# Output gates of the mLSTM heads computed as Strassen pairs in the gate stage, in a one-core diffusion step

## The chip, the cores and the metric

The kernel runs on one core of a Trainium2 chip. The metric is the device time of one execution in microseconds (us). Engines are named as in the profile: PE is the matrix engine (PEld its weight loads), DVE the vector engine, ACT the scalar engine, POOL the general one, SP the one whose queue issues most loads.

## The reference

One step of a layer for 256 context tokens and 1024 latent tokens, all fp32, model width 1024, four mLSTM heads of 128:

```python
u = rmsnorm(x, g_norm1) * (1 + sc1) + sh1
proj = u @ w_in
xp, su, sv, q, k, v, o_pre, gate_pre, br_pre = jnp.split(proj, points, axis=-1)
y_a = pool_branch(xp, w_pool, pool_scale, grid)
y_b = sgu_branch(su, sv, g_sgu, w_sgu, b_sgu)
y_c, C_out, n_out, m_out = mlstm_branch(q, k, v, o_pre, gate_pre, ...)
branches = jnp.einsum('btrc,rcd->btrd', ys, w_branch)
gates = jax.nn.sigmoid(br_pre).reshape(B, T, N_BRANCH, D_MODEL)
merged = jnp.sum(gates * branches, axis=2)
x = x + gt1 * (merged @ w_out)
...
# at the end of mlstm_branch: h is the sum of both scans' rows, per head
h = h * lax.rsqrt(jnp.mean(h * h, axis=-1, keepdims=True) + EPS) * g_mlstm
y = jax.nn.sigmoid(o_pre) * h
```

After that come the feed-forward block (`relu(...)^2`) and a last RMSNorm. What matters here is `sigmoid(o_pre)`, the output gate of the heads: 512 columns of `w_in`, one block of 128 for each head, over 1280 tokens.

## The kernel before

All 1280 tokens lie along the free axis, in three groups: 512, 512 and 256 (`GROUPS`; the last holds the context). An fp32 product is made from three matmuls on split operands: hi·hi, hi·lo and lo·hi. So a plain projection of one block of 128 columns (`proj`, `dense`) takes 8 k-tiles x 3 = 24 matmuls for each group, 72 in all: 48 of 128x512 and 24 of 128x256 (L123 to L125).

The larger products of the layer are made in pairs of column blocks by a Strassen scheme (`Pair`, L910 to L912): 7 products of four k-tiles for the 1024 latent tokens, which are read as sums prepared once (`us`), and plain products for the context group. `GatePair` does it for the 24 column blocks of the branches' gates, in 12 pairs: its results get a sigmoid (`done`, L992) and are stored to DRAM (`scr_g`), where the merge reads them back.

The stages, in order of the code: adaLN and norm; gating scans; the four heads (about 80 to 450 us); the SGU's `sv` and the pooling windows (450 to 576); gate pairs (576 to 877); merge (877 to 1150); output projection, feed-forward, last norm.

A head (`head(h, kT, vT, qT)`) first transposes k and v (tk, tv), forms the states of both scans (kv, L596; L607), and then goes over the three groups. In each: `st` (k·q, L627) and `rb` (rows of the gating broadcast to all partitions, L631) on PE; for each of the two directions DVE adds masks (L635), ACT takes Exp (L637, L643) and DVE multiplies (L638, L645) to the weights w and e; `pv` multiplies them with v and the state (L654, L656); ACT and DVE normalise (L659 to L663) and ACT squares (L664); POOL takes the power -0.5 (L130), ACT scales (L670), PE transposes to `th` (L671), DVE writes `yc` (L673) and it is stored to DRAM (`scr_yc`). At the first group of each head, the output gate's projection `p_o` is made for all three groups (L669) and evicted on ACT by a sigmoid into `so` (L617).

A scheduler sets the order of the instructions on each engine from its own model of the time; instructions of different heads and of the later `sv` projections (L698 to L702, in blocks of 24 matmuls of 128x256 for each 128 tokens) are interleaved with a head's chain. PSUM tiles of projections come from one ring of three (`mm`), those of attention from one of five (`sd`). Weights of a projection are loaded raw, cast to hi on ACT (L93) and split to lo on DVE or POOL (L94).

After each gate pair, up to six pieces of the second modulation (`mod_piece`, 64 in all, on DVE, POOL and DMA; L541) are inserted: pair n may bring the count to 6n.

The merge reads the rows of one branch after the other (`yr`, order SGU, pool, mLSTM), splits them to hi and lo (ACT, DVE), and multiplies with `w_branch` (pb, L1070 to L1072); DVE multiplies with the gate and adds up (L1074 to L1077).

Of the kernel before, what the change touches and what calls it, by code (L numbers as in the profile page):

```python
# [7 lines left out]
F32 = mybir.dt.float32  # L8
# [40 lines left out]
def hybrid_step(  # L49
# [503 lines left out]
    vaug = z[:, 1280:2570].rearrange("p (c t) -> p c t", t=129)  # L553
    vs = z[:, 2570:5150].rearrange("p (c d t) -> p c d t", d=2, t=129)
    S = z[:, 5150:7730].rearrange("p (c d t) -> p c d t", d=2, t=129)
    so = z[:, 7730:9010]
    hn2 = [z[:, 9010 + i * 512 : 9522 + i * 512].rearrange("p (c t) -> p c t", t=P) for i in range(2)]

    def proj(idx, name, evict, eng=V, w=None, groups=range(3)):
        w = w or load_w(w_in[idx], name, eng=eng)  # L560
        for g in groups:
            ps = ps_mm(f"p_{name}{g}")
            dense(ps, w, uT, g)
            evict(g, ps)
# [10 lines left out]
    def head(h, kT, vT, qT):  # L575
# [36 lines left out]
            V.scalar_tensor_tensor(fin[:, d, :], S[:, nx, d, :], dc(nx, d), kv(nx, d), ALU.mult, ALU.add)  # L612
        A.dma_start(st_out[h], fin)

        def ev_o(g, ps):
            t0, n = GROUPS[g]
            A.activation(so[:, t0 : t0 + n], ps[:, :n], AF.Sigmoid)  # L617

        ssq = small([P, 16], f"ssq{h}")
        for g in range(3):  # L620
            t0, n = GROUPS[g]
            c0, ncn = t0 // P, n // P
            hn = hn2[(3 * h + g) % 2]
            st = ps_sd(f"st{h}_{g}")
            for c in range(ncn):
                s = slice(c * P, (c + 1) * P)
                PE.matmul(st[:, s], kT[g][:, s], qT[g][:, s], start=True, stop=True)  # L627
            pw, qw = [], []
            for d in range(2):
                rb = ps_sd(f"rb{h}_{g}_{d}")  # L630
                PE.matmul(rb[:, :n], selr[:, d * 4 + h : d * 4 + h + 1].to_broadcast([100, P]), rhl[g][0:100, :n], start=True, stop=True)  # L631
                w = tmp(f"w{h}_{g}_{d}")
                for c in range(ncn):
                    s = slice(c * P, (c + 1) * P)
                    V.scalar_tensor_tensor(  # L635
                        w[:, s], rb[:, s], GC[:, c0 + c, d * 4 + h : d * 4 + h + 1], masks[d], ALU.add, ALU.add)
                A.activation(w[:, :n], w[:, :n], AF.Exp)  # L637
                V.tensor_tensor(w[:, :n], w[:, :n], st[:, :n], ALU.mult)  # L638
                pw.append(w)
                e = tmp(f"e{h}_{g}_{d}")  # L640
                for c in range(ncn):
                    s = slice(c * P, (c + 1) * P)
                    A.activation(  # L643
                        e[:, s], rb[:, s], AF.Exp, bias=mpb[:, d * 4 + h, c0 + c : c0 + c + 1], scale=1.0)
                V.tensor_tensor(e[:, :n], e[:, :n], qT[g][:, :n], ALU.mult)  # L645
                qw.append(e)
            for cl in range(ncn):
                c = c0 + cl
                s = slice(cl * P, (cl + 1) * P)
                pv = ps_sd(f"pv{h}_{c}")  # L650
                pvv = pv[:, 0:258].rearrange("p (d t) -> p d t", t=129)
                for d in range(2):
                    inter = not (c == 8 and d == 0) and not (c == 9 and d == 1)
                    PE.matmul(pvv[:, d, :], pw[d][:, s], vaug[:, c, :], start=True, stop=not inter)  # L654
                    if inter:
                        PE.matmul(pvv[:, d, :], qw[d][:, s], S[:, c, d, :], start=False, stop=True)  # L656
                den = small([P, 2, 1], f"den{h}_{c}")
                em = EM[:, c, :].rearrange("p (d h) -> p d h", d=2)[:, :, h]
                A.activation(den[:, :, 0], pvv[:, :, P], AF.Abs)  # L659
                V.tensor_tensor(den[:, :, 0], den[:, :, 0], em, ALU.max)  # L660
                V.reciprocal(den, den)
                A.activation(hn[:, cl, :], pvv[:, 0, 0:P], AF.Copy, scale=den[:, 0, :])
                V.scalar_tensor_tensor(hn[:, cl, :], pvv[:, 1, 0:P], den[:, 1, :], hn[:, cl, :], ALU.mult, ALU.add)  # L663
                A.activation(vs[:, c, 0, 0:P], hn[:, cl, :], AF.Square, accum_out=ssq[:, c : c + 1])  # L664
            r = rstd_of(ssq[:, c0 : c0 + ncn], ncn, f"h{h}_{g}")
            if g == 0:
                proj(I_O + h, f"o{h}", ev_o)
            ps = ps_sd(f"th{h}_{g}")
            for cl in range(ncn):  # L669
                A.activation(hn[:, cl, :], hn[:, cl, :], AF.Copy, scale=r[:, cl : cl + 1])  # L670
                PE.transpose(ps[:, cl * P : (cl + 1) * P], hn[:, cl, :], ident)  # L671
            yc = tmp(f"yc{h}_{g}")
            V.scalar_tensor_tensor(  # L673
                yc[:, :n], ps[:, :n], ccol[:, C_GM + h : C_GM + h + 1], so[:, t0 : t0 + n], ALU.mult, ALU.mult)
            SP.dma_start(scr_yc[h, :, t0 : t0 + n], yc[:, :n])

    qkv = head_proj(0)
# [308 lines left out]

    ORDER = (1, 0, 2)
    scr_g = [[dp.tile([P, T], F32, name=f"scr_g{r}_{d}") for d in range(KT)] for r in range(3)]

    class GatePair(Pair):  # L990
        def done(self, t):
# [2 lines left out]
        def context_done(self, t, ps):  # L994
            A.activation(t, ps, AF.Sigmoid)

        def store(self, r, d):
            for f, (t1, t2) in enumerate(((self.a1, self.a2), (self.b1, self.b2))):
                dst = scr_g[r][d + f]
                A.dma_start(dst[:, 0:512], t1)  # L1000
                A.dma_start(dst[:, 512:1024], t2)
                A.dma_start(dst[:, 1024:1280], self.hc[:, f * 256 : f * 256 + 256])

    for kk in range(4):
        us["B11", kk], us["B21", kk], us["B22", kk] = uT[kk][0], uT[kk + 4][0], uT[kk + 4][1]
    NGP = 3 * KT // 2
    gates = {}

    def gate_pair(n):
        r, d = ORDER[n // 4], n % 4 * 2  # L1010
        i = I_BR + r * KT + d
        odd = n % 2
        gates[n] = GatePair(
            f"g{n}", n, (w_in[i], w_in[i + 1]), 8 if odd else 0, (4, 5, 6, 7) if odd else (14, 15, 18, 19), us, [uT[k][2] for k in range(KT)])
# [11 lines left out]
    for n in range(NGP):  # L1026
        if n not in gates:
            gate_pair(n)
            gates[n].begin()
            gates[n].contexts()  # L1030
        gates[n].rest()
        gates[n].store(ORDER[n // 4], n % 4 * 2)
        del gates[n]
        while n > 0 and piece < 64 and piece < 6 * n:
            mod_piece(piece, zs((12, 13, 16, 17)[piece % 4]))
            piece += 1

# [7 lines left out]
    for ri, r in enumerate(ORDER):  # L1045
        scr = (scr_ya, scr_yb, scr_yc)[r]
        ys = [[] for _ in range(4)]
        for g in range(3):
            for kc in range(4):
                t0, n = GROUPS[g]  # L1050
                raw = tmp2(f"yr{r}_{kc}_{g}")
                SP.dma_start(raw[:, :n], scr[kc, :, t0 : t0 + n])
                hi, lo = split_part(f"y{r}_{kc}", g)
                A.copy(hi, raw[:, :n])
                V.tensor_tensor(lo, raw[:, :n], hi.bitcast(F32), ALU.subtract)
                ys[kc].append((hi, lo))
# [499 lines left out]
```

## Time and profile before

| | |
|---|---|
| median of three runs | 1944.16 us (1943.91 to 1946.34) |
| profiled execution, its own time | 1943.31 us |
| its span | 1941.3 us |
| PE busy | 1908.4 us (98%) |
| DVE, ACT, POOL busy | 1287.9, 856.7, 382.1 us |
| mean granted clock of PE | 0.996 |

The span is from the first to the last instruction; 2.0 us of the execution lie around it. PE is near full from beginning to end, so a group's busy time on another engine says little by itself; what is to be looked for is where PE waits, and what stands on PE between two steps of a chain on the other engines.

### The profile page before, as it was taken

How to read it: one execution, taken by the hardware profiler on the slowest of the kernel's cores; microseconds unless marked ns; L12 is line 12 of the kernel's file. 1: busy time of each engine (PE TensorE's matmuls, PEld its weight loads, DVE VectorE, ACT ScalarE, POOL GpSimd, SP SyncE). 2: the span in 40 equal slices, each digit the busy share in tenths (PEclk: the TensorE clock that was granted, in tenths of full speed). 3: DMA queues.
4: the chain of work that ended last, by engine and by line, in shares of the span. 5: the costliest groups of instructions: out<-in, count | busy, mean ns of one | idle time of the engine just before them, and what ended most of it. 6: DMA issues, size and time to landing. Idle time of an engine off the chain costs nothing.

```text
span 1941.3 us, 28162 instructions
## 1 busy us (share of the span) xinstructions
PE 1908.4 (98%) x10166; PEld 1632.5 (84%) x10166; DVE 1287.9 (66%) x2200; ACT 856.7 (44%) x1760; POOL 382.1 (20%) x381
## 2 busy tenths in 40 slices
PE   8999999999999999999999999999999999999998
PEld 5878888998788888888888888888888888888886
DVE  6574443447759899875675599887876655754665
ACT  6444454653243333343123375555454544443443
POOL 1100001108202424230000005554431210000003
PEclk9999999999999999999999999999999999999999
DMA  9210111012635445459532435777774596654444
GB/s 370 77 60 33 45 38 39 28 57 68 204 125 168 151 151 161 157 195 328 164 103 98 151 121 200 275 263 264 250 256 139 193 335 203 210 168 152 165 133 160
DMA packets 149318, 313.33 MB, mean 161 GB/s; under 512 B 17550, under 2 KB 40818, under 8 KB 147130
## 3 DMA queue, kind: packets, MB, share of 16 engines
q1 hardware_dynamic: 107354, 220.73, 34.6%
q0 software_dynamic: 15520, 57.75, 7.8%
q10 hardware_dynamic: 26304, 33.04, 4.7%
q8 instruction: 80, 1.31, 0.3%
q14 instruction: 60, 0.49, 0.1%
HBM read 217.59 MB, written 93.36 MB: 160 GB/s over the span
## 4 chain that ended last, share of the span: by engine, by line
PE 87%; DVE 6%; ACT 2%; issue 2%; DMA 2%; POOL 1%; SPq 0%; ACTq 0%; POOLq 0%; DVEq 0%
PE w L1423 6%; PE w L1424 6%; PE w L1425 6%; PE fT L912 3%; PE fT L910 3%; PE fT L911 3%; PE pb L1071 3%; PE pb L1070 3%; PE pb L1072 3%; PE fB L911 2%; PE fB L910 2%; PE fB L912 2%; PE fT_g L912 2%; PE fT_g L910 2%; PE fT_g L911 2%; PE po L1190 2%
## 5 line engine op out<-in xcount | busy, mean ns | idle before, releaser
L1262 POOL TENSOR_TENSOR z<-z 128x512 f32<-128x512 f32 x64 | 100.6, 1572 | 119.6 <-DMA z<-in_w_ff 110.1
L967 DVE TENSOR_TENSOR z<-z 128x512 f32<-128x512 f32 x112 | 94.2, 841 | 2.5
L547 POOL PARTITION_ALL_REDUCE acc<-acc x16 | 54.4, 3435 | 183.4 <-DVE acc L541 114.3
L541 DVE SCALAR_TENSOR_TENSOR acc<-z,scond,acc 128x512 f32<-128x512 f32 x112 | 84.6, 803 | 0.1
L1377 POOL TENSOR_TENSOR rs_y<-rs_y,neghalf 128x1 f32<-128x1 f32 x10 | 9.7, 967 | 332.2 <-DVE rs_y L1376 332.1
L1228 ACT ACTIVATE z<-z 128x512 f32<-128x512 f32 x64 | 40.5, 632 | 75.7 <-DVE z L976 38.4
L992 ACT ACTIVATE z<-z 128x512 f32<-128x512 f32 x48 | 30.3, 632 | 54.2 <-DVE z L976 20.6
L130 POOL TENSOR_TENSOR rs_h<-rs_h,neghalf 128x4 f32<-128x4 f32 (+1 forms) x12 | 10.9, 909 | 200.0 <-DVE rs_h L129 199.8
L673 DVE SCALAR_TENSOR_TENSOR yc<-th,ccol,z 128x512 f32<-128x512 f32 (+1 forms) x12 | 7.9, 661 | 58.4 <-PE th L671 58.4
L1076 DVE TENSOR_TENSOR sg<-pb,sg 128x512 f32<-128x512 f32 (+1 forms) x48 | 28.8, 601 | 26.6 <-PE pb L1072 26.4
L901 ACT CAST hi_wb<-raw_wb 128x512 fp32r<-128x512 f32 x24 | 14.7, 620 | 64.0 <-PE pb L1071 37.9
L1229 ACT ACTIVATE z<-z 128x512 f32<-128x512 f32 x64 | 40.3, 629 | 1.1
L1191 DVE TENSOR_TENSOR po<-po,gt 128x512 f32<-128x512 f32 (+1 forms) x24 | 14.6, 609 | 35.6 <-PE po L1190 31.2
L548 POOL TENSOR_TENSOR acc<-acc,bt 1x512 f32<-1x512 f32 x16 | 26.2, 1651 | 59.1 <-issue 59.1
L1253 POOL DMA_DIRECT2D scr_s<-x x48 | 26.3, 550 | 52.4 <-DVE x L1247 46.6
L758 POOL TENSOR_TENSOR z<-z 128x1024 f32<-128x1024 f32 (+13 forms) x20 | 33.6, 1702 | 7.7 <-ACT z L742 5.4
L1194 ACT ACTIVATE po<-z 128x512 f32<-128x512 f32 (+1 forms) x24 | 12.7, 530 | 48.6 <-DVE z L1193 34.3
L607 DVE SCALAR_TENSOR_TENSOR z<-z,dmb,kv 128x129 f32<-128x129 f32 x56 | 16.6, 345 | 21.8 <-PE kv L596 21.3
L1077 DVE TENSOR_TENSOR z<-z,sg 128x512 f32<-128x512 f32 (+1 forms) x48 | 28.7, 602 | 1.2
L660 DVE TENSOR_TENSOR den<-den,gcol 128x2 f32<-128x2 f32 x40 | 6.2, 160 | 31.0 <-ACT den L659 29.9
L130 POOL TENSOR_TENSOR rs_f<-rs_f,neghalf 128x4 f32<-128x4 f32 (+1 forms) x3 | 3.3, 1092 | 116.9 <-DVE rs_f L129 116.9
L654 PE MATMUL pv<-z,w 128*128 128x129 f32 x160 | 25.1, 275 | 0.9 <-DVE w L638 0.9
(5142 smaller groups left out, 7274.1 us busy)
## 6 DMA issues: line engine op xcount, KB each, us to landing
z<-in_w_ff SPq DMA_DIRECT2D x64, 512.0 KB, 5.3
z<-in_w_ada SPq DMA_DIRECT2D x64, 256.0 KB, 3.4
scr_t<-z POOLq DMA_DIRECT2D x16, 1024.0 KB, 4.3
z<-in_w_in SPq DMA_DIRECT2D x24, 512.0 KB, 4.3
scr_g<-z ACTq DMA_DIRECT2D x48, 256.0 KB, 2.0
sg<-scr_g SPq DMA_DIRECT2D x48, 256.0 KB, 4.5
scr_h<-z ACTq DMA_DIRECT2D x48, 256.0 KB, 3.5
scr_s<-x POOLq DMA_DIRECT2D x48, 256.0 KB, 3.8
```

Of the source, the lines that this page charges most:

```text
L541: V.scalar_tensor_tensor(acc[j], raw, scond[:, k, j : j + 1], acc[j], ALU.mult, ALU.add)
L910: PE.matmul(ps, whi[:, s], ahi, start=first and k == ks[0], stop=False)
L911: PE.matmul(ps, whi[:, s], alo, start=False, stop=False)
L912: PE.matmul(ps, wlo[:, s], ahi, start=False, stop=end and k == ks[-1])
L967: V.tensor_tensor(out, x, y, op)
L1070: PE.matmul(pb[:, :n], whi[:, s], yh, start=kc == 0, stop=False)
L1071: PE.matmul(pb[:, :n], whi[:, s], yl, start=False, stop=False)
L1072: PE.matmul(pb[:, :n], wlo[:, s], yh, start=False, stop=kc == 3)
L1262: G.tensor_tensor(out, x, y, ALU.subtract)
L1423: PE.matmul(banks[j], h_[:, s], rh, start=fp == 0, stop=False)
L1424: PE.matmul(banks[j], l_[:, s], rh, start=False, stop=False)
L1425: PE.matmul(banks[j], h_[:, s], rl, start=False, stop=fp == NFP - 1)
```

## The change

The projection of the output gates leaves the heads. Their four column blocks are made as two further `GatePair`s, numbers 12 and 13, after the 12 of the branches, with the same sigmoid and a store to DRAM (`scr_o`). In the heads `yc` is now only scaled by `g_mlstm`, on ACT instead of DVE. Where the merge reads the rows of the last branch (r = 2, mLSTM), it loads the gate too and DVE multiplies it in ahead of the split. The pieces of modulation go five to a pair instead of six.

```diff
-    so = z[:, 7730:9010]
...
-        def ev_o(g, ps):
-            t0, n = GROUPS[g]
-            A.activation(so[:, t0 : t0 + n], ps[:, :n], AF.Sigmoid)
...
             r = rstd_of(ssq[:, c0 : c0 + ncn], ncn, f"h{h}_{g}")
-            if g == 0:
-                proj(I_O + h, f"o{h}", ev_o)
...
             yc = tmp(f"yc{h}_{g}")
-            V.scalar_tensor_tensor(
-                yc[:, :n], ps[:, :n], ccol[:, C_GM + h : C_GM + h + 1], so[:, t0 : t0 + n], ALU.mult, ALU.mult)
+            A.activation(yc[:, :n], ps[:, :n], AF.Copy, scale=ccol[:, C_GM + h : C_GM + h + 1])
...
+    scr_o = [dp.tile([P, T], F32, name=f"scr_o{h}") for h in range(H)]
...
-        def store(self, r, d):
+        def store(self, dsts):
...
-                dst = scr_g[r][d + f]
+                dst = dsts[f]
...
-    NGP = 3 * KT // 2
+    GATES = [(I_BR + r * KT + d, scr_g[r][d : d + 2]) for r in ORDER for d in range(0, KT, 2)]
+    GATES += [(I_O + h, scr_o[h : h + 2]) for h in range(0, H, 2)]
+    NGP = len(GATES)
...
-        while n > 0 and piece < 64 and piece < 6 * n:
+        while n > 0 and piece < 64 and piece < 5 * n:
...
+                if r == 2:
+                    so = tmp2(f"so{kc}_{g}")
+                    SP.dma_start(so[:, :n], scr_o[kc][:, t0 : t0 + n])
+                    V.tensor_tensor(raw[:, :n], raw[:, :n], so[:, :n], ALU.mult)
```

The code behind it is the same, but the scheduler's order in the heads is not. Below are three places in head 2. In a row stand the line, the operation, what it writes and reads, the shape; names carry head and group (`rb2_2_0`: head 2, group 2, direction 0; `pv2_8`: head 2, block of tokens 8) and a running number.

PE around the second transposition and the last group, before. Between the first row of `sv0_3` and the last shown of `sv0_4` stand 40 more of the two.

```order
L671 MATMUL th2_1_2990<-cst_78,z_76 128x128
L627 MATMUL st2_2_3002<-kq2_2362 128x128 x2
L631 MATMUL rb2_2_0_3005<-rhl2_1167,selr_1171 128x256
L631 MATMUL rb2_2_1_3016<-rhl2_1167,selr_1171 128x256
L671 MATMUL th2_1_2990<-cst_78,z_76 128x128 x3
L698 MATMUL sv0_3_3856<-hi_sv0_0_3761,u0h0_384 128x256
...
L700 MATMUL sv0_4_3884<-lo_sv0_1_3768,u5h1_827 128x256
L654 MATMUL pv2_8_3027<-z_76,w2_2_0_3007 128x129
L654 MATMUL pv2_9_3038<-z_76,w2_2_0_3007 128x129
L656 MATMUL pv2_9_3038<-z_76,e2_2_0_3012 128x129
```

The same place after:

```order
L664 MATMUL th2_1_2738<-cst_78,z_76 128x128
L622 MATMUL st2_2_2750<-kq2_2194 128x128 x2
L626 MATMUL rb2_2_0_2753<-rhl2_1167,selr_1171 128x256
L626 MATMUL rb2_2_1_2764<-rhl2_1167,selr_1171 128x256
L664 MATMUL th2_1_2738<-cst_78,z_76 128x128 x3
L649 MATMUL pv2_8_2775<-z_76,w2_2_0_2755 128x129
L649 MATMUL pv2_9_2786<-z_76,w2_2_0_2755 128x129
L651 MATMUL pv2_9_2786<-z_76,e2_2_0_2760 128x129
L649 MATMUL pv2_8_2775<-z_76,w2_2_1_2766 128x129
L649 MATMUL pv2_9_2786<-z_76,w2_2_1_2766 128x129
L651 MATMUL pv2_8_2775<-z_76,e2_2_1_2771 128x129
L690 MATMUL sv1_0_3727<-hi_sv1_0_3717,u0h0_384 128x256
```

The 42 `sv` matmuls between rb and pv are gone, and `sv1_0`, one block of 24, stands between pv and the next th. At groups 0 and 1 of head 2 likewise one block of 24 is left on each side of pv (`sv0_6` to `sv0_9`), where 34 to 40 matmuls of `p_q`, `p_o` and `sv` stood.

ACT between the normalisation of head 2's group 1 and its scaling, before:

```order
L662 ACTIVATE z_76<-pv2_7_2975,den2_7_2980 128x128
L664 ACTIVATE z_76,ssq2_2721<-z_76 128x128
L701 COPY vn1_3799<-sv0_1_3800 128x256
L664 ACTIVATE z_76,ssq2_2721<-z_76 128x128
L702 ACTIVATE sv0_1_3800,vsq_3758<-sv0_1_3800 128x256
L664 ACTIVATE z_76,ssq2_2721<-z_76 128x128 x2
L670 ACTIVATE z_76<-z_76,rs_h2_1_2987 128x128 x4
```

And after, with the first rows of what follows:

```order
L657 ACTIVATE z_76<-pv2_7_2723,den2_7_2728 128x128
L659 ACTIVATE z_76,ssq2_2553<-z_76 128x128
L93 CAST hi_sv1_1_3723<-raw_sv1_1_3721 128x1024
L659 ACTIVATE z_76,ssq2_2553<-z_76 128x128 x3
L93 CAST hi_xp3_4017<-raw_xp3_4015 128x1024
L663 ACTIVATE z_76<-z_76,rs_h2_1_2735 128x128 x4
L666 ACTIVATE yc2_1_2747<-th2_1_2738,ccol_74 128x512
L632 ACTIVATE w2_2_0_2755<-w2_2_0_2755 128x256
```

Two casts of weights stand among the Squares instead of an eviction of `sv`, and `yc` (L666) stands ahead of the next group's Exp (L632).

POOL in head 2, before:

```order
L130 TENSOR_TENSOR rs_h2_0_2805<-rs_h2_0_2805,neghalf_81 128x4
L94 TENSOR_TENSOR lo_sv1_0_4054<-raw_sv1_0_4051,hi_sv1_0_4053 128x1024
L130 TENSOR_TENSOR rs_h2_1_2987<-rs_h2_1_2987,neghalf_81 128x4
L130 TENSOR_TENSOR rs_h2_2_3049<-rs_h2_2_3049,neghalf_81 128x2
L94 TENSOR_TENSOR lo_sv1_1_4060<-raw_sv1_1_4057,hi_sv1_1_4059 128x1024
```

And after:

```order
L130 TENSOR_TENSOR rs_h1_2_2183<-rs_h1_2_2183,neghalf_81 128x2
L130 TENSOR_TENSOR rs_h2_0_2637<-rs_h2_0_2637,neghalf_81 128x4
L94 TENSOR_TENSOR lo_sv1_1_3724<-raw_sv1_1_3721,hi_sv1_1_3723 128x1024
L130 TENSOR_TENSOR rs_h2_1_2735<-rs_h2_1_2735,neghalf_81 128x4
L130 TENSOR_TENSOR rs_h2_2_2797<-rs_h2_2_2797,neghalf_81 128x2
```

The split of `sv1_1` stands ahead of the power of group 1, where the split of `sv1_0` stood.

More of the change, by code (lines that the diff above doesn't have):

```diff
@@ L1005, in hybrid_step @@
         us["B11", kk], us["B21", kk], us["B22", kk] = uT[kk][0], uT[kk + 4][0], uT[kk + 4][1]
-    NGP = 3 * KT // 2
     gates = {}
+    GATES = [(I_BR + r * KT + d, scr_g[r][d : d + 2]) for r in ORDER for d in range(0, KT, 2)]
+    GATES += [(I_O + h, scr_o[h : h + 2]) for h in range(0, H, 2)]
+    NGP = len(GATES)
     def gate_pair(n):
-        r, d = ORDER[n // 4], n % 4 * 2
-        i = I_BR + r * KT + d
+        i = GATES[n][0]
         odd = n % 2
@@ L1031, in hybrid_step @@
         gates[n].rest()
-        gates[n].store(ORDER[n // 4], n % 4 * 2)
+        gates[n].store(GATES[n][1])
         del gates[n]
-        while n > 0 and piece < 64 and piece < 6 * n:
+        while n > 0 and piece < 64 and piece < 5 * n:
             mod_piece(piece, zs((12, 13, 16, 17)[piece % 4]))
```

## The prediction

> **What bounds the kernel now.** I read the page first (engine totals, the chain), then PE's waits, then windows by stage, then single stretches of the head stage.
>
> ```profile
> span 1941.3 us, 28162 instructions
> PE 1908.4 (98%) x10166; PEld 1632.5 (84%) x10166; DVE 1287.9 (66%) x2200; ACT 856.7 (44%) x1760; POOL 382.1 (20%) x381
> PE 87%; DVE 6%; ACT 2%; issue 2%; DMA 2%; POOL 1%; SPq 0%; ACTq 0%; POOLq 0%; DVEq 0%
> ```
>
> PE is busy for 98% of the span and is 87% of the chain that ended last; only 33 us of the span are not its own. So a change is worth what it takes from or adds to PE's instruction stream, plus every stall that it opens or closes in that stream.
>
> ```profile
> 140.00:450.00 310.00, 307.15 (x2049) 280.00 (x2048) 134.05 (x391) 161.56 (x470) 30.41 (x27) 1.00 0.13 42
> 575.90:877.00 301.10, 298.08 (x1571) 256.62 (x1571) 259.92 (x371) 113.45 (x208) 98.21 (x60) 1.00 0.51 166
> 877.00:1150.00 273.00, 273.00 (x1451) 235.93 (x1450) 175.71 (x320) 89.94 (x183) 10.08 (x16) 1.00 0.47 157
> ```
>
> Columns: length of the stretch, busy PE, PEld, DVE, ACT, POOL, granted clock, DMA share, GB/s. The three are the head stage, the gate pairs and the merge. PE fills each (2.9, 3.0 and 0 us short). In the head stage that is not because attention is short of dependencies: PE is kept busy by projections standing between an attention step and the next. In the gate stage DVE is the next engine (260 of 301); in the merge it has 97 us free.
>
> ```profile
> PE fT_g L912 <- DVE s_g7l L893: 1.7, 1, 1.7
> PE sv L698 <- ACT sv L702: 1.2, 1, 1.2
> PE p_xp L123 <- DVE mt L842: 1.1, 1, 1.1
> PE p_k L123 <- ACT kT L349: 0.7, 1, 0.7
> PE p_k L123 <- ACT z L617: 0.7, 1, 0.7
> ```
>
> These are the waits in PE's list that the change could touch (total, times, longest).
>
> **PE's arithmetic.**
>
> ```profile
> 100.55:114.33 13.78, 13.78 (x72) 11.84 (x72) 0.00 (x0) 1.00 0.28 91
> 177.08:185.72 8.64, 8.64 (x38) 6.95 (x38) 0.00 (x0) 1.00 0.16 63
> ```
>
> First row: one head's whole output-gate projection on PE, 72 matmuls in 13.78 us (48 of 128x512, 24 of 128x256). Second: 38 of 128x512 in 8.64 us, so 0.227 each; then a 128x256 takes (13.78 - 48 x 0.227)/24 = 0.12. Removed: four heads, 192 wide and 96 narrow. Added: two pairs; a pair is 7 products of 12 wide matmuls plus 48 narrow ones, so 168 wide and 96 narrow. Net -24 x 0.227 = **-5.4 us**. Cross-check: 12 pairs in 298.08 us are 24.84 each, against 2 x 13.78 = 27.56 for two heads the old way, 2 x 2.72 = 5.4. Since PE is full in both places, this term is the surest of the sum.
>
> **The cover that goes.** Between two attention steps PE waits for a chain. Chain A: from the first rb matmul through masks, Exp and multiply to w and e, which pv reads. Chain B: from the last pv through the normalisation, Squares, POOL's power and the scaling to the th transposes.
>
> ```profile
> 240.78 0.71 PE L631 MATMUL rb<-rhl,selr 100*128 100x512 f32 x2
> 243.36 0.68 DVE L638 TENSOR_TENSOR w<-w,st 128x512 f32<-128x512 f32 x1
> 245.70 0.69 DVE L645 TENSOR_TENSOR e<-e,qT 128x512 f32<-128x512 f32 x1 [0.27 <-ACT e L643]
> 432.64 0.48 PE L631 MATMUL rb<-rhl,selr 100*128 100x256 f32 x2
> 434.46 0.42 DVE L638 TENSOR_TENSOR w<-w,st 128x256 f32<-128x256 f32 x1
> ```
>
> Chain A is 244.04 - 240.78 = 3.3 us to the first w (5.6 to the last e) for a 512-token group, and 2.2 for the 256-token one.
>
> ```profile
> 193.15:196.89 3.74, 3.74 (x34) 3.73 (x33) 2.24 (x9) 1.78 (x7) 0.00 (x0) 1.00 0.23 26
> 196.89:200.51 3.62, 3.62 (x18) 2.99 (x17) 1.43 (x7) 1.88 (x12) 1.02 (x1) 1.00 0.39 136
> 290.29:293.50 3.21, 3.21 (x15) 2.63 (x15) 1.21 (x7) 1.57 (x9) 0.70 (x1) 1.00 0.59 163
> 352.60:356.99 4.39, 3.17 (x27) 2.96 (x26) 1.82 (x11) 3.02 (x16) 1.01 (x1) 1.00 0.06 15
> 354.00 0.40 ACT L701 COPY vn<-sv 128x256 f32<-128x256 f32 x1
> 354.56 0.41 ACT L702 ACTIVATE sv<-sv 128x256 f32<-128x256 f32 x1
> 355.24 0.33 ACT L664 ACTIVATE z<-z 128x128 f32<-128x128 f32 x1
> 356.99 1.28 ACT L670 ACTIVATE z<-z,rs_h 128x128 f32<-128x128 f32 x4 [1.33 <-POOL rs_h L130]
> ```
>
> The first stretch is the 16 pv matmuls of a wide group with the few records between them; the next three run from a last pv to the first scaling (L670): chain B is 3.6 to 4.4 us for 512 tokens, 3.2 for 256, and a first scaling of 0.3 goes on top before th can start. In the 4.39 us of head 2 PE already fell short (3.17 busy), and an sv eviction (L701, L702) stood on ACT among the Squares (L664).
>
> Before, 34 to 42 matmuls of p_o, of later k, v, q and of sv stand in each of these places of head 2 (in heads 0 and 1 as many, of k, v, q and p_o). The new order pulls the later heads' projections forward one after the other to fill the places that p_o leaves. Heads 0 and 3 keep their cover. From the end of head 1 through head 2 what is left is one sv group of 24 narrow matmuls, 24 x 0.12 = 2.9 us, or nothing. Place by place (stall = chain minus what stands in it):
> - head 1, group 2, rb to pv: only three th transposes (about 0.3). ACT must first finish the scaling and the new yc, then Exp: 2.4 after rb, minus 0.5: 1.9. Then chain B 3.2 + 0.3 against one sv group: 0.7.
> - the start of head 2 (tk, kv), where an sv group waits for an mm buffer whose eviction stands in ACT's queue behind the head's work: 1.1.
> - head 2, group 0: chain B at 4.4 (evictions of sv stand among the Squares, as in the row at 352.60) + 0.4 against 2.9: 2.0.
> - head 2, group 1: the same chain 4.0 + 0.3, and ACT now has the cast hi_sv1_1 after the first Square and POOL the split lo_sv1_1 ahead of the power:
>
> ```profile
> L93 ACT CAST hi_sv<-raw_sv 128x1024 fp32r<-128x1024 f32 x4 | 4.2, 1052 | 3.4 <-PE sv L699 1.7 <-PE p_v L124 0.9 <-PE p_o L124 0.8
> L94 POOL TENSOR_TENSOR lo_sv<-raw_sv,hi_sv 128x1024 fp32r<-128x1024 f32 x4 | 9.6, 2393 | 52.1 <-ACT hi_sv L93 52.1
> ```
>
> The cast costs the Squares 1.05; the split's 2.39 outlasts the three Squares left (0.33 each) by about 1.4, and the power waits behind it on POOL. So 6.8 against 2.9: 3.9.
> - head 2, group 2: 1.9 as in head 1, 0.8 until the next sv group has a buffer, 0.6 at th; then 0.3 at head 3's first kv.
>
> Sum **+13.2 us**. Bounds: with the short chains (3.3, 3.2, 3.6) and the cast and split early, 6; with the long chain B of 4.4 in every place and the cast and split fully in line, 17.
>
> **Waits that go.** p_k on the p_o eviction goes with it (0.7); the sv and kT waits sit where the order is new, and go (1.2 + 0.7): **-2.6**, between 0 and -2.6.
>
> **ACT and DVE in the heads.**
>
> ```profile
> L617 ACT ACT_TABLE_LOAD x10 | 12.8, 1283 | 1.5 <-DVE z L446 1.4
> L637 ACT ACT_TABLE_LOAD x9 | 11.5, 1283 | 2.5 <-DVE fin L612 2.4
> L673 DVE SCALAR_TENSOR_TENSOR yc<-th,ccol,z 128x512 f32<-128x512 f32 (+1 forms) x12 | 7.9, 661 | 58.4 <-PE th L671 58.4
> L785 ACT ACTIVATE ya<-pp,ccol 128x512 f32<-128x512 f32 x8 | 5.4, 688 | 28.4 <-PE pp L783 27.9 <-DVE z L800 0.5
> ```
>
> Sigmoid and Exp alternate on ACT in every head, with 19 table loads, 24.3 us. With the sigmoid gone from the heads they go nearly all, and that helps chain A wherever a load stood in it; the chains above are taken without one, so the gain is already in the sum and isn't counted twice. The Trainium skill (ScalarE: Activation LUTs, "What ACT_TABLE_LOAD costs") adds a drain of 1380 ns to the load's 1283 ns. The rows agree on the load; by that rule 19 x 2.66 = 51 us of ACT would go, in an engine with 148 us idle in the head stage, so the sum would stay the same. The new yc takes 0.69 on ACT (form of L785) instead of 0.66 to 0.75 on DVE: nothing by itself, but in group 2 it stands ahead of Exp, which is counted above.
>
> **Gate stage.** Pieces of the modulation are spread over 13 pairs at five each instead of six, so DVE is lighter per pair; of the wait of 1.7 at pair 7 and smaller ones I take **-1.0**, between -3.0 (all that PE lacks there) and +1. Sigmoid is the only table there.
>
> **Pool stage.** p_xp waits 1.1 for DVE now. That wait should go; but sv matmuls are drawn forward out of this place, so less PE work covers the pool windows: **-0.5**, between -1.1 and +2.5.
>
> **Merge, queues.**
>
> ```profile
> scr_g<-z ACTq DMA_DIRECT2D x48, 256.0 KB, 2.0
> yr<-scr_yc SPq DMA_DIRECT2D x8, 256.0 KB, 4.4
> ```
>
> The last branch gets 12 loads on SP's queue, each some 4.4 us to land as its neighbours of the same size, and 12 multiplies, about 0.7 by the wide form: 8 us of DVE in a stage with 97 free. They are issued ahead of the last branch's products, so 0; at worst one load and one multiply are seen once, +5. PE has no gap there, so nothing can be won. The two pairs' 12 stores join 72 like them on ACT's queue, where nothing waits for them; their four weight loads are the ones that leave SP's queue in the heads: 0.
>
> **Sum.** -5.4 + 13.2 - 2.6 - 1.0 - 0.5 = +3.7 us. The profiled execution took 1943.31 us (span 1941.3 and 2.0 around it), 0.85 below the median of the runs, 1944.16; on the median the forecast is 1947.9, rounded to **1948**.
>
> **Rivals.**
> 1. *The cover is enough, and the saving comes through.* The place that decides is head 2: if the stalls sum to under 8 us, the 5.4 + 2.6 + 1.5 of the other terms more than pay for them. For it: the table loads leave ACT's queue, chains without one are 3.3 and 3.6, and evictions of sv can slip into ACT's idle time. Against it: 2.9 us of filler is shorter than the shortest chain B that any row shows. With 0 to 8 us of stalls the time is between 1944.16 - 9.5 = 1934.7 and 1942.7, likeliest with 5: 1939.6.
> 2. *The stalls slow the clock.*
>
> ```profile
> PE pc L498 <- DVE z L486: 3.6, 1, 3.6
> 131.05:137.88 6.83, 6.26 (x35) 5.83 (x36) 6.75 (x22) 2.70 (x4) 0.00 (x0) 0.50 0.05 12
> 1155.20:1158.46 3.26, 0.26 (x2) 0.26 (x3) 2.44 (x7) 2.42 (x6) 0.70 (x1) 1.00 0.32 124
> 1158.46:1161.88 3.42, 3.34 (x16) 2.79 (x15) 2.12 (x7) 3.15 (x9) 0.00 (x0) 0.50 0.75 238
> ```
>
> After PE waited 3.6 us the granted clock was 0.50 for 6.83 us; after a stretch of 3.26 us with 0.26 busy, for 3.42 us. Half speed over one such stretch costs 1.7, over two 3.4. The stall of 3.9 at head 2, group 1, is long enough; those of 2 are not. Its price with 2 us more of stalls in the pool stage: 1948 + 1.7 to 3.4 + 2 = 1951.7 to 1953.4. The Trainium skill (TensorE: Matmul & The Clock Gate, "Part 1: The HAM clock gate") has the half rate follow an idle window of about 3.4 us on a free-running grid. The rows agree in length (3.42, and 6.83 is two); by that rule only stalls that fill a whole window count, so 3.9 us would seldom, while the row at 1155.20 shows it after 3.26 us not wholly idle. The rule lowers this rival's chance, the row keeps it.
> 3. *Nothing changes that can be measured*, because the second pairs' saving lies beside something else after all, and the stalls stay as small: 1944.
>
> **How the numbers follow.** A difference of 0.2%, 3.9 us, is about what a measurement of this kernel can tell from none; that puts faster under 1940.3 and slower over 1948.05. Forecast (stalls of 9.5 to 17, clock kept): chance 0.48, 1944 to 1952, about a third of it within the bound: same 0.16, slower 0.32. Rival 1: 0.28, faster 0.16, same 0.12. Rival 2: 0.20, slower 0.19, same 0.01. Rival 3: 0.04, same. Together faster 0.16, same 0.33, slower 0.51. The range of the forecast alone is 1944 to 1952; for eight in ten it goes from 1938.5 (rival 1 without its best part) to 1956 (rival 2 with the stalls at their bound).
>
> **What would show it.** In the changed profile: PE busy about 5 us lower in all; PE's waits longest at th and pv on the scaling and on w in head 2, over 10 us together, with the longest at head 2, group 1; about 19 fewer table loads; two more pairs of 24.8 us; no wait on the loads of the gates in the merge. It is wrong if the th and pv waits sum to under 8 us, if stalls appear in head 0, 1 or 3, or if DVE becomes late in the merge.

## The result and the profile after

| kernel | median of runs | profiled execution | its span | clock |
|---|---|---|---|---|
| before | 1944.04 us (1941.41 to 1946.34, 6 runs) | 1943.31 us | 1941.3 us | 0.996 |
| after | 1951.62 us (1949.20 to 1956.44, 6 runs) | 1949.20 us | 1947.4 us | 0.993 |

After to before is 1.0042, 95% interval 1.0031 to 1.0053: slower by 7.6 us. The profile is of one execution, the lowest of the six; its span is 6.1 us longer than the one of before (the span of a second profile of the same kernel, further down, is 7.8 us longer). First the page after: the span, the engine totals and the granted clock in 40 slices (the fourth row is that clock before):

```profile
span 1947.4 us, 28196 instructions
PE 1910.0 (98%) x10142; PEld 1632.4 (84%) x10142; DVE 1301.5 (67%) x2234; ACT 848.8 (44%) x1771; POOL 380.8 (20%) x381
PEclk9999998999999999999999999999999999999999
PEclk9999999999999999999999999999999999999999
```

PE has 24 matmul records fewer, and yet is not less busy (1910.0 against 1908.4): the third row has a dip in the seventh slice, at 292 to 341 us, where the matmuls ran slower. That is head 2. The first three of the next rows are PE's waits between head 0 and head 3 before, the next four those after; then one between the first and the last gate pair after, and at the feed-forward's start, behind the merge, the two longest before and after (total, times, longest):

```profile
PE sv L698 <- ACT sv L702: 1.2, 1, 1.2
PE pv L654 <- DVE w L638: 0.9, 1, 0.9
PE p_k L123 <- ACT kT L349: 0.7, 1, 0.7
PE th L664 <- ACT z L663: 6.3, 3, 4.5
PE pv L649 <- DVE w L633: 3.3, 2, 1.6
PE sv L690 <- ACT sv L694: 0.6, 2, 0.4
PE p_q L123 <- ACT vT L349: 0.4, 1, 0.4
PE fB_g L904 <- DVE a_g0l L885: 0.4, 1, 0.4
PE fc L912 <- DVE a_0l L893: 1.4, 1, 1.4
PE fT L912 <- DVE s_0l L893: 0.8, 1, 0.8
PE fT L904 <- DVE s_2l L885: 0.9, 1, 0.9
PE fc L902 <- ACT hc L1230: 0.7, 1, 0.7
```

The heads now wait 10.6 us where they had waited 2.8; the gate pairs 0.4 where they had waited 3.4. In the merge the list is empty before and after. (The merge's own products run from 859 to 1027 us before; the stretch of 877 to 1150 given for it ahead of the result takes in most of the output projection.)

To see all of it, I took from each trace the distance of each matmul's start to the next one's, less the median of its shape in that trace (0.227 us for 128x512 and so on), and summed it by stage. This counts waits and slow clock together, in us (the stages end at 165, 450, 559, 859 and 1027 us before, at 164, 417, 514, 858 and 1028 after):

```
             up to      heads   pooling  gate    merge  rest   sum
             head 0                      pairs
before       21.2        4.2      6.3     4.8     0.3    9.3   45.9
after        20.2       15.6      5.2     1.3     0.3   14.0   56.5
after again  21.3       15.7      5.0     0.9     0.3   15.1   58.2
```

("after again" is the second profile of the same kernel, below.) 56.5 - 45.9 = +10.6, less the 5.4 of the removed arithmetic, is +5.2 of the 6.1. (The median of rb rose from 0.27 to 0.32 us; with before's medians for both, the heads after are 16.7 and about 1 us more is accounted for.) The heads lost 11.4; gate pairs and pooling gained 4.6; the rest lost 4.7, 3.6 of it at the feed-forward's start and 1.2 further into it, and that was in no step of the prediction.

The worst place, head 2, group 1, in the timeline after (start, length, engine, line, operation):

```profile
323.24 1.07 ACT L93 CAST hi_sv<-raw_sv 128x1024 fp32r<-128x1024 f32 x1
324.39 2.34 POOL L94 TENSOR_TENSOR lo_sv<-raw_sv,hi_sv 128x1024 fp32r<-128x1024 f32 x1 [11.80 <-ACT hi_sv L93]
324.97 0.22 ACT L659 ACTIVATION_READ_ACCUMULATOR z<-z 128x1 f32 x1
325.22 1.54 DVE L129 TENSOR_SCALAR rs_h<-ssq 128x4 f32<-128x4 f32 x1 [1.57 <-ACT z L659]
326.84 1.91 POOL L130 TENSOR_TENSOR rs_h<-rs_h,neghalf 128x4 f32<-128x4 f32 x1
328.78 1.28 ACT L663 ACTIVATE z<-z,rs_h 128x128 f32<-128x128 f32 x4 [2.66 <-POOL rs_h L130]
329.24 0.47 PE L664 MATMUL th<-cst,z 128*128 128x128 f32 x1 [4.53 <-ACT z L663]
```

The cast stands before the last three Squares, whose sums are read by 325.19. POOL is then still at the split (to 326.73), the power starts at 326.84, and PE has stood for 4.53 us. And the clock around it (columns as in the prediction):

```profile
324.19:327.60 3.41, 0.52 (x5) 0.32 (x3) 2.38 (x2) 1.93 (x8) 3.10 (x2) 1.00 0.00 0
327.60:337.84 10.24, 6.97 (x31) 6.60 (x32) 4.06 (x15) 5.46 (x20) 1.15 (x1) 0.50 0.35 128
```

A stretch with 0.52 us of PE work is followed by three of 3.41 us at half clock. 6.97 us of matmuls ran in them, so 3.5 us of PE time were lost, as far as no later wait hides it.

### The profile page after: what moved, and what is told of

It is laid out like the page before. It is cut to its first block, busy times and chain, and to the rows that moved or that the text cites. A ratio compares the mean times of both kernels' runs of the same rounds, so it can differ in the third digit from the quotient of the medians.

```text
span 1947.4 us, 28196 instructions
## 1 busy us (share of the span) xinstructions
PE 1910.0 (98%) x10142; PEld 1632.4 (84%) x10142; DVE 1301.5 (67%) x2234; ACT 848.8 (44%) x1771; POOL 380.8 (20%) x381
## 4 chain that ended last, share of the span: by engine, by line
PE 65%; DMA 8%; POOL 4%; DVE 4%; issue 2%; ACT 1%; SPq 0%; POOLq 0%; ACTq 0%; DVEq 0%
PE w L1421 6%; PE w L1422 6%; PE w L1423 6%; DMA z<-in_w_ff 4%; POOL z L1260 3%; PE pb L1068 3%; PE pb L1069 3%; PE pb L1070 3%; DMA scr_t<-z 3%; PE fT_g L904 2%; PE fT_g L902 2%; PE fT_g L903 2%; PE po L1188 2%; PE po L1186 2%; PE po L1187 2%; PE fB_g L902 2%
## 5 line engine op out<-in xcount | busy, mean ns | idle before, releaser
L1226 ACT ACTIVATE z<-z 128x512 f32<-128x512 f32 x64 | 40.5, 632 | 71.4 <-DVE z L968 38.8
L985 ACT ACTIVATE z<-z 128x512 f32<-128x512 f32 x56 | 35.3, 632 | 64.0 <-DVE z L968 18.6
L630 DVE SCALAR_TENSOR_TENSOR w<-rb,gcol,cst 128x128 f32<-128x128 f32 x80 | 21.8, 344 | 35.5 <-PE rb L626 35.5
L1227 ACT ACTIVATE z<-z 128x512 f32<-128x512 f32 x64 | 40.3, 629 | 1.1
L750 POOL TENSOR_TENSOR z<-z 128x256 f32<-128x256 f32 (+13 forms) x20 | 37.6, 1888 | 12.7 <-ACT z L735 6.2
L588 DVE TENSOR_TENSOR z<-tv,gcol 128x512 f32<-128x512 f32 (+1 forms) x24 | 14.4, 602 | 18.2 <-ACT z L585 17.9
```

The lines of the kernel that those rows point to most:

```text
L1226: A.activation(t, t, AF.Relu)
```

## The experiments

All are timed against the kernel before on the same chip; a ratio has its 95% interval. Splits are the lo parts of weights. One thing goes for nearly all of them: the edit also changes the scheduler's order behind the merge. Of PE's 4448 rows there, 192 stand otherwise than in the change when sv's splits are on DVE, 29 with matmuls in the wait, 24 with yc on DVE; none when the count of pieces is six. So part of a difference in time can lie there, and the table's "rest" is given where it matters.

**The change again.** No edit.

> The change itself once more, beside the other runs. Both theories: ratio to before 1.0042 within its interval (1.0031 to 1.0053); waits at th and pv in head 2 as in its first profile, the clock halved after the wait at head 2, group 1.

1.0036 (1.0024 to 1.0049), median 1952.15 us. The waits in the heads were the same to 0.01 us; the clock halved at the same place. So the waits go with the order, not with one execution.

**Splits of sv on DVE.**

```diff
-        wq = [load_w(w_sv[q, hf], f"sv{q}_{hf}", eng=G) for hf in range(2)]
+        wq = [load_w(w_sv[q, hf], f"sv{q}_{hf}", eng=V) for hf in range(2)]
```

> The change, with the lo splits of the four sv weights on DVE instead of POOL; PE's order in the heads stays as in the change. Theory (the loss is the thin cover in head 2, worst at group 1, where POOL's split stands ahead of the power): the power no longer waits behind a split of 2.34 us; DVE's split takes about 1.2, so the scaling starts 1 to 2 us earlier and PE's wait at th of head 2, group 1, falls from 4.5 to 2.7 to 3.5 us; if it is then too short to slow the clock, another 3.2 us come back. Time 1 to 5 us under the change's 1951.6, ratio to before 1.0016 to 1.0037. Rival (the loss lies in the feed-forward and merge, the head's waits are hidden elsewhere): the wait shrinks but the ratio stays at 1.004.

> The change with sv's splits on DVE once more, beside the three others. Ratio to before within 0.9986 and 1.0003 as it was; if it comes out near 1.002, the gain of 9 us was one of a few placements of the clock's stretches, and only the 2 us of the shorter wait are sure.

0.9994 (0.9986 to 1.0003) and 1.0006 (0.9997 to 1.0015): against the change's 1.0042 and 1.0036 some 7.6 us better, by one argument in one line, and level with before, not faster than it. The first profile at head 2, group 1:

```profile
327.18 1.23 DVE L94 TENSOR_TENSOR lo_sv<-raw_sv,hi_sv 128x1024 fp32r<-128x1024 f32 x1 [0.63 <-ACT hi_sv L93]
328.33 0.16 DVE L129 TENSOR_SCALAR rs_h<-ssq 128x4 f32<-128x4 f32 x1
328.57 1.01 POOL L130 TENSOR_TENSOR rs_h<-rs_h,neghalf 128x4 f32<-128x4 f32 x1 [13.28 <-DVE rs_h L129]
PE th L664 <- ACT z L663: 4.4, 3, 2.6
```

The wait fell from 4.5 to 2.6 us, much as the theory had it (2.7 to 3.5). Two things make it up: from the last sum of the Squares to the start of the power it is 0.5 us instead of 1.65, and the power itself takes 1.01 instead of 1.91. But the gain is larger than the 1 to 5 us expected. In the table above, the second of its profiles has heads 12.4, rest 12.3, sum 53.0: 3.5 to 5.2 under the change's two, with the half clock still there (for 6.83 us instead of 10.24). The first, of the slowest of its 12 runs, has 12.8, 11.9 and 55.0. So 1.7 to 3.2 us of the gain lie behind the merge, where the order is another one: the ratio did not stay, so the rival is out as it stood, but a part of the loss does lie there. What the medians show beyond 3.5 to 5.2 isn't accounted for by a single profile.

**The same splits in the kernel before.** The same edit there.

> The kernel before, with the lo splits of the four sv weights on DVE instead of POOL, and nothing else. Theory (the split costs only where the chain behind it has no cover; before, 35 sv or p_o matmuls stand there): ratio 0.999 to 1.001. Rival (splits on DVE are 5 to 9 us better by themselves, whatever covers the chain): 0.995 to 0.9975, and then the change would still lose against it.

1.0010 (1.0001 to 1.0019). The theory's side: where the chain is covered the split's engine is worth nothing (if anything, DVE is the worse place: the gate pairs come to 6.2 us against 4.8 in the table's measure). The rival is out.

**Matmuls inside the wait.**

```diff
+            if h == 2 and g == 1:
+                dm = ps_sd("dm")
+                for cl in range(ncn):
+                    for j in range(4):
+                        PE.matmul(dm[:, 0:129], hn[:, cl, :], vaug[:, c0 + cl, :], start=True, stop=True)
             ps = ps_sd(f"th{h}_{g}")
```

> The change, with 16 extra matmuls of the form 128x129 (1.8 us of PE work whose result nobody reads) between the pv and the th of head 2, group 1; they read the normalised rows as these are finished, so they lie inside PE's wait of 4.5 us and leave the chain as it is. Theory (that wait costs twice: itself, and a half clock for three stretches of 3.41 us afterwards): the clock stays at 1.00 from 329 to 338 us, th starts when it did, and the time is 2 to 3.3 us under the change's: ratio 1.0025 to 1.0032. Rival (the half clock after it is no consequence of this wait, or costs nothing that counts): ratio 1.004 as in the change, or more by the added work.

1.0016 (1.0005 to 1.0026). The 16 matmuls took 3.73 us, as 32 records, so two passes each, and th started within 0.02 us of where it did in the change, counted from its sv block:

```profile
326.20 3.73 PE L665 MATMUL dm<-z 128*128 128x129 f32 x32
330.91 0.33 PE L669 MATMUL th<-cst,z 128*128 128x128 f32 x1 [0.97 <-ACT z L668]
```

The clock stayed at 1.00 until 333.3 us and was halved for one stretch only, after the next wait. The median moved the theory's way by about 4 us; but in the profile the heads come to 11.0 + 3.7 of added work = 14.7, only 0.9 under the change's 15.6, since a th wait of 0.8 us appears behind it; the rest is 14.7, as in the change. So it is shown that the wait slows the clock; that the slow clock costs the full 3.5 us is not.

**The same with the splits on DVE.** 8 matmuls instead of 16, and the edit to the splits.

> The change with sv's splits on DVE, and 8 extra matmuls of 128x129 whose result nobody reads inside the remaining wait of 2.6 us at th of head 2, group 1 (1.9 us of PE work, two passes each as the run with 16 showed 3.73 us). Theory (a stretch of 3.41 us in which PE is busy under about 1.5 us halves the clock for the next): no half clock in the heads after the gating scans; 0 to 3 us under the run without them, ratio 0.9978 to 0.9994. Rival (the wait alone counts): the same as without them, 0.9994, or above.

1.0004 (0.9995 to 1.0013), beside 1.0006 without them, timed together: no difference that can be told. The clock did what was expected (mean 0.996 instead of 0.993, no half clock in the heads):

```profile
330.00:340.00 10.00, 7.74 (x62) 7.10 (x61) 4.37 (x16) 7.34 (x29) 0.69 (x1) 1.00 0.27 92
330.00:340.00 10.00, 8.37 (x51) 7.86 (x50) 3.94 (x15) 6.20 (x25) 0.70 (x1) 0.66 0.28 98
```

(First row with them, second without.) At full clock PE gets 62 matmuls done instead of 51, and waits more: 2.3 us of 10 instead of 1.6. So the slow clock was partly free here, in a stretch that waits for chains anyway. The rival, that the wait counts and the clock little, is nearer here.

**yc back on DVE.**

```diff
-            A.activation(yc[:, :n], ps[:, :n], AF.Copy, scale=ccol[:, C_GM + h : C_GM + h + 1])
+            V.tensor_scalar(yc[:, :n], ps[:, :n], ccol[:, C_GM + h : C_GM + h + 1], None, ALU.mult)
```

> The change, with yc scaled on DVE instead of ACT. Theory (yc stands ahead of the next group's Exp in ACT's queue where PE has no filler): PE's wait from rb to pv at the last groups of heads 1 and 2 falls from 1.6 us each to about 0.9; nothing else moves: 1 to 2 us less, ratio 1.003 to 1.004. Rival (Exp waits for the masks on DVE anyway, and yc on DVE now delays those): the waits stay at 1.6 or grow, ratio 1.004 to 1.005.

1.0045 (1.0033 to 1.0058). The time and the waits come out as the rival had them:

```profile
279.68 0.75 DVE L666 TENSOR_SCALAR yc<-th,ccol 128x512 f32<-128x512 f32 x1 [2.96 <-PE th L664]
280.35 1.12 DVE L630 SCALAR_TENSOR_TENSOR w<-rb,gcol,cst 128x128 f32<-128x128 f32 x4
282.00 0.68 PE L649 MATMUL pv<-z,w 128*128 128x129 f32 x4 [2.36 <-DVE w L633]
280.99 0.42 ACT L632 ACTIVATE w<-w 128x256 f32<-128x256 f32 x1 [1.86 <-DVE w L630]
277.26 1.12 DVE L630 SCALAR_TENSOR_TENSOR w<-rb,gcol,cst 128x128 f32<-128x128 f32 x4 [3.24 <-PE rb L626]
277.71 0.69 ACT L666 ACTIVATE yc<-th,ccol 128x512 f32<-128x512 f32 x1 [1.27 <-PE th L664]
278.29 0.41 ACT L632 ACTIVATE w<-w 128x256 f32<-128x256 f32 x1
330.82 1.13 DVE L630 SCALAR_TENSOR_TENSOR w<-rb,gcol,cst 128x128 f32<-128x128 f32 x4 [2.94 <-PE rb L626]
331.67 0.69 ACT L666 ACTIVATE yc<-th,ccol 128x512 f32<-128x512 f32 x1 [1.61 <-PE th L664]
332.26 0.41 ACT L632 ACTIVATE w<-w 128x256 f32<-128x256 f32 x1
```

In the first four rows (head 1, this run) yc stands ahead of the masks on DVE, and pv waits 2.36 us; in the change (the next three rows, head 1; the last three, head 2) DVE starts the masks as soon as rb is there and pv waits 1.63. The theory's mechanism is in the rows all the same: from the start of the masks to the first Exp (L632) it is 0.64 us with yc on DVE, 1.03 and 1.44 in the change, where Exp starts as yc ends. So yc on ACT holds Exp up by 0.4 and 0.8 us; on DVE it holds the masks up by more, about 1.0 us from the end of rb (279.31) to their start. A version with yc behind Exp wasn't tried.

**Half of the change, heads 0 and 1.** One pair instead of two.

```diff
-    GATES += [(I_O + h, scr_o[h : h + 2]) for h in range(0, H, 2)]
+    GATES += [(I_O + h, scr_o[h : h + 2]) for h in MOVED[::2]]
...
+            if g == 0 and h not in MOVED:
+                proj(I_O + h, f"o{h}", ev_o)
```

> Half of the change: only the gates of heads 0 and 1 are made as a pair (number 12) and multiplied in at the merge; heads 2 and 3 keep their projection, sigmoid and yc as before; six pieces of modulation to a pair. Saves 2.7 us of PE. Theory (what counts is not how much is moved but which attention steps are left without work between them): the order has nothing between rb and pv, pv and th of head 2, group 0, and among its 18 kv; stalls of about 3, 4 and 2 us and a clock drop of 3: 5 to 11 us over before, ratio 1.0025 to 1.0055. Rival (the loss goes with the amount moved): half of the whole change's, ratio 1.002.

1.0037 (1.0025 to 1.0049). Half of the change loses as much as the whole, and not where the whole does:

```profile
PE th L671 <- ACT z L670: 4.2, 1, 4.2
PE pv L654 <- DVE w L638: 2.8, 2, 2.6
PE sv L702 <- ACT z L617: 1.5, 1, 1.5
```

The two longest waits (4.2 and 2.6 us) lie in head 2, group 0, where the new order left nothing between rb and pv and between pv and th; the clock was halved for 10.24 us after them. Another 4.4 us are waits of up to 1.5 at kv, sv and pv of head 2. The heads come to 16.2 in the table's measure, the rest to 9.6, near the 9.3 of before. It is not the amount moved that counts.

**Half of the change, heads 1 and 3, splits on DVE.** The pair is made of heads 1 and 3; the rest as in the half above.

> Half of the change, with sv's splits on DVE: the gates of heads 1 and 3 are made as one pair and multiplied in at the merge, heads 0 and 2 keep projection, sigmoid and yc as before; six pieces of modulation a pair. Saves 2.7 us of PE. Theory: of the change's waits only those at head 2, groups 1 and 2, remain (2.6 and 1.6 us, and 0.8 at its last th): ratio 0.9985 to 1.001, unlike the half with heads 0 and 1, which was 1.0037. Rival (half of the whole change's loss wherever it is taken from): 1.002.

1.0009 (1.0000 to 1.0017). The waits in the heads are those of head 2, groups 1 and 2, 2.5 and 2.4 us (the second one while the clock was halved), beside one of 0.4. The heads come to 9.4 in the table's measure, the rest to 12.0. So the waits are where the theory had them, but for the one of 0.8. Whether the place alone makes the time better than with heads 0 and 1 is not shown, since the splits are on DVE too; but in the chain behind the 4.2 us of the half above no split stood on POOL (the power took 1.0 us and began 0.1 after DVE's half of it). And the rival's 1.002 was half of the loss with the splits on POOL: against the whole change with its splits on DVE (0.9994 and 1.0006) the time does not tell the two apart.

**Wide filler kept for head 2.** The first ten sv blocks are written ahead of head 3's projections, with their splits on DVE.

```diff
+        if h == 2:
+            sv_load(0)
...
+            sv_here(h, g, "pv")   # blocks of sv, in tiles of ps_mm
...
+            sv_here(h, g, "th")
```

> The change, with the first ten sv blocks written ahead of head 3's projections in the program (the split of sv's weights on DVE as in the run before): the scheduler then spends the narrow sv blocks in heads 0 and 1 and leaves the wide k, v, q of head 3 (24 x 0.227 = 5.4 us a group instead of 2.9) for head 2. Theory (what costs is the length of what stands in each place, and stretches with PE under half busy slow the clock): four to five waits of 1.2 to 1.6 us, none over 2, sum 6 to 8 against 10.3, clock kept in the heads; 5 to 9 us under the change, ratio 0.999 to 1.001. Rival (the total of the waits is given by the chains, they only move to head 1): sum 10 again, ratio 1.002 to 1.004.

1.0035 (1.0023 to 1.0046). The rival is right:

```profile
PE th L666 <- ACT z L665: 5.2, 3, 2.5
PE pv L650 <- DVE w L633: 3.3, 2, 1.6
PE sv L689 <- ACT kq L349: 1.3, 1, 1.3
```

The narrow blocks were spent in head 1 and the waits went there (th 1.4 and 2.5 in head 1, 1.3 in head 2; pv 1.6 in each): 10.7 us, as in the change. Shifting the cover moved the waits. The clock was not kept either: it was halved for 6.83 us after the th wait of 2.5. The rest came to 17.7, the most of all runs.

**sv held in the heads.** All twenty sv blocks are written into heads 0 and 1, in tiles of the attention ring, splits on DVE.

```diff
+        if h in (0, 1):
+            sv_load((0, 1).index(h))
...
+            sv_chunk(q, i, ps_sd)
```

> The change, with all twenty sv blocks written into heads 0 and 1, two or one in each place between rb, pv and th, in PSUM tiles of the attention ring so that they cannot be drawn forward (splits on DVE). Heads 1 and 3 are covered everywhere, head 2 by wide projections. Only 15.1 us of PE work are left between head 3's last th and the first pooling product, by the matmul durations of the trace before, against 24.7 in the change and 35.8 before. Theory (PE work that covers chains is a fixed stock from the heads through the pooling; the change took 55 us out of it): waits in the heads under 4 us in all, but 8 to 11 us at the first pooling product, with the clock halved after it: ratio 1.001 to 1.005. Rival (only the heads lacked cover, the pooling chain is short enough): waits under 4 in all, ratio 0.995 to 0.997.

1.0183 (1.0169 to 1.0197), 35 us slower than before, far outside of both expectations. Two places:

```profile
PE mx L847 <- DVE vn L723: 9.4, 5, 3.3
118.93:131.44 12.51, 0.00 (x1) 0.02 (x1) 12.24 (x13) 3.52 (x3) 1.07 (x2) 0.58 0.05 15
```

The first is about what the theory gave for the end of the heads (8 to 11), though it shows at the products of the SGU (mx) and not at pooling's. The second I had not seen: in the change 72 matmuls of head 1's k and 62 of its v stand ahead of the pc matmuls, which wait for the gating scans; here, with the sv weights ahead of them in the weight ring, only those of k do, and PE stood 12.5 us behind DVE (4.4 in the change). In the table's measure that is 39.9 up to head 0 and 17.5 in the pooling, where the change has 20.2 and 5.2. The heads did not come to under 4 us either: PE waited 4.1 us in head 0, not in head 1, 2.9 in head 2 and 2.5 in head 3. The run shows that the matmuls which cover one chain are taken from another; it doesn't show a version that gains.

**Six pieces of modulation a pair.**

```diff
-        while n > 0 and piece < 64 and piece < 5 * n:
+        while n > 0 and piece < 64 and piece < 6 * n:
```

> The change, with up to six pieces of modulation after each gate pair, as before, instead of five. Theory (DVE is the next engine in the gate stage; before, its pieces made PE wait 3.4 us there, in the change 0.4): waits of 2 to 3 us on DVE return between the 7th and 11th pair: ratio 0.001 over the change's. Rival (the waits went because of the two further pairs or another order, not the number of pieces): the same time as the change, waits under 1 us.

1.0041 (1.0027 to 1.0055) beside 1.0036 of the change: the intervals cover one another, so the time says nothing. The trace does:

```profile
PE fT_g L904 <- DVE s_g10l L885: 1.1, 1, 1.1
PE fT_g L904 <- DVE s_g9l L885: 0.2, 1, 0.2
PE fT_g L904 <- DVE s_g8l L885: 0.2, 1, 0.2
```

With six, waits on DVE come back at pairs 8 to 10, 1.5 us in all where 2 to 3 were expected, and the gate pairs come to 3.7 in the table's measure (change 1.3 and 0.9, before 4.8). Most of the gain in this stage belongs to the five.

## Why the prediction was right, step by step

The direction and the range held; 1951.6 lies 3.6 us above the forecast of 1948, at the upper end of 1944 to 1952. That it lies inside is partly luck: the forecast had the clock kept, and it was not, so that what happened is rival 2 in its main part, priced at 1951.7 to 1953.4 with 2 us of stalls in the pool stage that did not come; and two misses upward, the clock and the feed-forward, met two downward, waits sized too large and gate pairs that gained more. By the sum's own terms:

- *PE's arithmetic, -5.4.* 24 wide matmuls fewer are in the trace; two pairs take the place of the 288 matmuls.
- *The cover that goes, +13.2.* Measured waits: 10.1 us at these places, and 0.4 at a p_q of head 1 that had no term. By place, forecast and measured: head 1, group 2: 1.9 and 1.63 at pv, 0.7 and 0.4 at th; start of head 2: 1.1 and 0.6 (two waits); head 2, group 0: 2.0 and 1.4; group 1: 3.9 and 4.5; group 2: 1.9 and 1.63, and no wait behind it (1.7 had been forecast there and at head 3). The mechanism and the places were right; the small ones were sized too large by 0.3 to 0.6 each. In group 1 the cast and the split cost about what was forecast; what comes on top is covered by the power, which took 1.91 us there, against a mean of 1.01 for its shape before. The reason given for 1.9, yc ahead of Exp, is in the rows, but is worth 0.4 to 0.8 of the 1.63.
- *Waits that go, -2.6.* The three named are gone (1.2, 0.7 and 0.7), and with them one of 0.9 at pv that the sum had not named.
- *Gate stage, -1.0.* Measured -3.5 (4.8 to 1.3; -3.9 in the second profile): mis-sized, and beyond the bound of -3.0; the run with six pieces shows that the count of pieces does most of it.
- *Pool stage, -0.5.* -1.1.
- *Merge, 0.* 0: no wait in the list, 12 multiplies of 7.2 us in all.
- *Table loads.* 24 fell to 5; the 19 forecast. What that was worth by itself isn't shown.
- *The clock.* Rival 2 came true as a part: half clock after head 2, group 1, in every profile of the change. 10.24 us of it took 3.5 us from PE, of which the runs with matmuls inside the wait recovered between nothing and 4.
- *What had no term:* the feed-forward, +4.7, most of it at its start. The scheduler's order differs there in a few dozen rows (casts, hc and the context's matmuls swapped), and PE waits on casts and splits for pairs that had been in time. Waits are 1.6 us of it; 1.4 come from the half clock behind the merge, which lasted 6.83 us in this profile and 3.41 before (and 3.41 in the change's second profile, whose rest is 15.1 all the same, with more waits). Three profiles with this order have a rest of 14.0, 15.1 and 12.8 (the last with six pieces), that of before and that of before with splits on DVE, whose order on PE differs in two rows there, 9.3 and 10.7. I had seen the difference in the order and put it at nothing without a row. This is the step that failed: it costs about as much as the arithmetic saves. Which of the swapped rows does it wasn't tried.
- *The signs.* The longest wait was where it had been put, the table loads and the merge as said. PE's busy time did not fall by 5 us but rose by 1.6: the half clock, longer than before, makes up about 4.6 of the difference; the rest isn't accounted for. The th and pv waits come to 9.6 us, over the 8 that were named as the limit, but only 7.5 of them in head 2, where over 10 had been expected. Stalls in head 1 were named as a sign of being wrong, and they came (2.4 us); but the list of places had itself put 2.6 there, so that this sign contradicted the sum.

The forecast of +3.7 and the measured +7.6 differ by the clock and the feed-forward, less the gate pairs and the oversized waits. This adds up only to the profiles, which are 6.1 and 7.8 us apart, and there within 1 to 2 us.

## What to carry to other kernels

Where an engine is full only because independent work stands between the steps of a chain, that work isn't free to move: count what is left in each place against the chain there, because half the move may cost as much as the whole. A weight split in an engine's queue ahead of a four-element operation can decide the longest wait; look for it before moving anything larger. And an order made by a scheduler changes far from the edit too: cost those places, however small the difference reads.

## What the runs showed of the hardware

The clock was halved also after stretches that were far from idle. I cut the 14 profiles, but for their last 15 us, into stretches of 3.41 us on the grid that the changes of the clock lie on. All 45 stretches at full clock that were followed by half clock had PE busy for 0 to 1.77 us, all but one of them up to 1.52; the lowest at full clock that was not followed by it had 1.70. (In the last 15 us two with 1.49 and 1.50 were not.) In these runs the boundary lies near half of 3.41. This goes for leaving full clock; at half clock another such stretch followed even where PE had been busy for all of 3.41 us, three times. Two rows from either side, each with its successor (splits on DVE, then before):

```profile
328.32:331.73 3.41, 1.34 (x10) 1.11 (x10) 2.13 (x6) 2.22 (x6) 1.01 (x1) 1.00 0.59 159
331.73:338.55 6.82, 5.51 (x26) 5.54 (x27) 3.22 (x13) 4.36 (x18) 0.12 (x1) 0.50 0.34 113
752.28:755.69 3.41, 1.70 (x9) 1.00 0.38 119
755.69:759.10 3.41, 3.41 (x17) 1.00 0.72 227
```

The first has two waits (2.6 and 1.6 us) with matmuls between them, none of them 3.41 long. By the Trainium skill (TensorE: Matmul & The Clock Gate, "Part 1: The HAM clock gate") the half rate comes after at least one idle window of about 3.4 us. These rows do not agree: a pair of short waits close together was enough.

DVE and POOL held each other up on small operations. The first half of the power, on DVE (L129), took 1.54 us and ended with POOL's split; with no split there it took 0.16. POOL's power took 1.91 us beside the following split on DVE, which had begun 0.17 us ahead of it and ended 0.87 us before it did; with no split beside it, it took 1.01:

```profile
326.67 1.21 DVE L94 TENSOR_TENSOR lo_xp<-raw_xp,hi_xp 128x1024 fp32r<-128x1024 f32 x1
```

(After; the other rows are those of head 2, group 1, after and with the splits on DVE.) By the Trainium skill (SBUF — State Buffer, "SBUF: two separate sides") the two engines share a pair of ports that one of them locks for a whole instruction. The trace agrees: an operation of four elements per partition lasted until the other engine's split was done (L129), or for about its usual time beyond that (the power). For the chain only the second adds: the power had to wait in POOL's queue until the split ended at 326.73, so that L129, which ended at 326.76, cost next to nothing more, while DVE's split of xp made the power 0.9 us longer.
